# A hybrid attention and DeltaNet layer: ones ahead, the norm row spread by TensorE, key products evicted by ScalarE, three more query pairs in seven products

## The chip, the cores and the metric

The kernel runs on one NeuronCore of a Trainium2 chip. The metric is the device time of one execution in microseconds (us), lower is better. Engines are named as in the profile: PE (TensorE, with PEld for its weight loads), DVE (VectorE), ACT (ScalarE), POOL (GpSimd), SP (SyncE, which issues nearly all DMAs).

## The reference

One decoder layer on 528 tokens (16 meta tokens ahead of 512) of width 1024, f32. One RMS norm feeds one big projection; two branches run beside each other on it, are gated, merged and projected back.

```python
h = concatenate([meta, x])                               # 528 x 1024
hn = rms_norm(h, norm_w)
aq, ak, av, az, dq, dk, dv, dz, db, da, ga, gd = split(hn @ w_in)
# attention branch: 8 heads, two softmaxes each, p0 - lam * p1, causal
y_a = (rms_norm(diff_attention(aq, ak, av)) * silu(az)) @ w_branch_attn
# delta branch: 8 heads; q, k, v by a causal convolution over 4 tokens and silu,
# q and k l2-normalised, gates beta and g, chunks with a triangular solve and a state
y_d = (rms_norm(gated_delta(q, k, v, beta, g)) * silu(dz)) @ w_branch_delta
out = rms_norm(h + (sigmoid(ga) * y_a + sigmoid(gd) * y_d) @ w_out, final_norm_w)[16:]
```

## The kernel before

All matrix products are done in three passes of a split: a value is a high part (rounded to the matmul's type) plus a low part, and high x high, high x low and low x high are summed. So each weight block of 128 output columns is loaded (`raw`, 512 KB), ACT casts its high part (`wh`) and DVE subtracts for the low part (`wl`); the normed input stands as `hnH` and `hnL`, features on partitions, tokens along the free axis.

**Start.** `loads` issues the DMAs on SP's queue: four tiles of x (`xt`, 128 tokens each), the norm row `nwb` broadcast to 128 partitions, the meta tokens (`mt`), and weight blocks between them. `normalise(n)` squares a tile on ACT (the sum is `ss`), DVE multiplies it by the norm row (`weigh`), POOL takes the power -1/2 (`rs`), DVE makes a diagonal `dg` of it, and PE transposes and scales the tile with matmuls against `dg` into PSUM banks; ACT casts to `hnH` and DVE subtracts to `hnL`. `first_products` multiplies the first two key blocks as soon as their tokens are there.

**Middle.** Four groups of two delta heads and two attention heads. `ORDER` (from `dense_order`) lists the weight blocks in the order in which PE takes them: keys, values and queries of the delta heads (dk, dv, dq), their gates (dz), and ak, av, aq, az of the attention heads. A single block takes 48 matmuls, 24 in each of two stretches of tokens, or 24 of 512 columns (`product`). Blocks named in `PAIRS` are taken two at a time (`pair_of_blocks`) by seven products of half size in place of eight (a Strassen-like scheme): sums of weights are built on DVE (`st`, `raw`, in `split_pair`), sums of the input (`sumH`, `sumL`) once at the start. This holds for ak with av, and from the second group for pairs of dk and of dv. After a block come a convolution on DVE (`xp`, `y`), tanh on ACT, and for the delta heads `delta_pair`: key products (`products`, into `MT`), query products (`queries`, into `AT`), a triangular solve (`ts`, `TM`, `square`), a state `S` carried over four chunks (`steps`), and the meta tokens' part of the state (`um`). `attention` does scores and softmax (`psc`, `e`). PSUM is six banks plus a double one `psc`; SLOTS and BANKS say how many buffers of each kind there are.

**End.** The two branch matrices in pairs, then `w_out` in 512-column products; `finish` adds the residual, squares (ACT), multiplies by the final norm row (`fnw`, DVE), takes a power (POOL), scales (ACT for the left half, DVE for the right) and stores. The last tile's right half comes in two pieces of 256.

The order of every engine's instructions is fixed when the program is built: a planner (`Plan`) runs the generators (each `yield` names an engine, an event or a buffer) on costs per instruction, and at each step takes the one that could start first, then the lower rank. `COLD` is the time until which it doubles the cost of PE's work. So an edit in one place moves instructions all over the program; nearly every instruction has source line L231, that of the recording helper, so the profile is read by tiles.

Of the kernel before, what the change touches and what calls it, by code (L numbers as in the profile page):

```python
# [18 lines left out]
P = 128  # L19
# [40 lines left out]
PAIRS = [n for n, (name, i) in enumerate(ORDER) if name == "ak" or name in ("dk", "dv") and i > 1 and i % 2 == 0]  # L60
# [19 lines left out]
COLD = 10500  # L80
# [185 lines left out]
def hybrid_block(ctx: ExitStack, tc: tile.TileContext, x, meta, wblk, wbd, wout, pcol, prow, out):  # L266
# [52 lines left out]
    nwb = mk(sp, [P, D], F32, "nwb")  # L319
# [178 lines left out]
    def loads():  # L498
        for n in range(1, NC + 1):
            yield SP  # L500
            S.dma_start(out=xt[n], in_=x[P * (n - 1):P * n, :])
            done(f"x{n}")
            if n == 1:
                yield SP
                S.dma_start(out=nwb, in_=prow[:, 1296:2320].broadcast_to([P, D]))
                done("nwb")
                yield SP
# [12 lines left out]
        for n in range(2, len(ORDER) + 8):  # L520
            yield from load_weights(n)
# [4 lines left out]
    def normalise(n):  # L526
# [3 lines left out]
        ss, rs, dg = (mk(sp, [P, k], F32, t, 3) for k, t in ((1, "ss"), (1, "rs"), (P, "dg")))  # L530
# [3 lines left out]
        def weigh():  # L534
            yield "nwb"
            yield DVE
            V.tensor_tensor(out=xt[n], in0=xt[n], in1=mt[:, P:2 * P] if n == 0 else nwb, op=ALU.mult)
            done(f"xw{n}")

        spawn(weigh())  # L540
        src = ss
        if n == 0:
# [4 lines left out]
            T.matmul(pt[:, 0:1], samb.rearrange("p k t -> p (k t)"), ss, start=True, stop=True)  # L547
            src = pt[:, 0:1]
# [10 lines left out]
        def part(pt, dst):  # L559
            yield ACT  # L560
            A.copy(out=hn[0][dst], in_=pt)
            tick(f"hh{n}", 1 if n == 0 else 2)
# [5 lines left out]
        for hf in range(1 if n == 0 else 2):  # L568
# [12 lines left out]
            spawn(part(pt, dst))  # L581
# [318 lines left out]

    def after_dq(h, banks):
        pair["q", h], _ = yield from conv_silu(banks, h, NM, "qT")
        give("y")
        done(f"dq{h}")
# [82 lines left out]
    def delta_pair(gi):  # L987
# [114 lines left out]
        def products(i):  # L1102
# [12 lines left out]
            for c in range(NC):  # L1115
                yield DVE
# [134 lines left out]
        yield name("scr")  # L1251
        msub = room[1].rearrange("p a t -> p (a t)")[:, 0:D].rearrange("p (j i) -> p j i", i=32)
# [41 lines left out]
        def meta_state():  # L1294
# [15 lines left out]
            for i in range(2):  # L1310
                yield DVE
                um.append(mk(dp, [32, P], F32, "um", 2))
                V.tensor_scalar_mul(out=um[i], in0=pm[0:32, 0:P], scalar1=ms[:, 4 + i:5 + i])
# [94 lines left out]
        def square(i):  # L1408
# [5 lines left out]
            yield DVE  # L1414
            V.tensor_copy(out=t64[64:128, 4 * i:4 * i + 4], in_=px[64:128])
# [6 lines left out]
            yield DVE  # L1422
            V.tensor_scalar_mul(out=TT[0:64, 4 * i:4 * i + 4, 64:128], in0=py[0:64], scalar1=-1.0)
# [222 lines left out]
    WHOLE = dict(dk=whole_dk, dv=whole_dv, ak=whole_ak, av=whole_av)  # L1646
# [165 lines left out]
    def first_products():  # L1812

        yield ("psc",)
        sc = bank("psc")
        dst = [[], (sc[:, 0, :], sc[:, 1, :])]
        for _ in range(2):
            yield ("pd",)
            dst[0].append(bank("pd"))
        banks = [Banks(n) for n in range(2)]  # L1820
        for hb, (t0, nn) in enumerate(FULL):
            for n in range(2):
                pd = dst[n][hb][:, :nn]
                for m, (i, j) in enumerate(((0, 0), (1, 0), (0, 1))):
                    yield (f"wh{n}", f"w{n}")[i]
                    for e in (0, 1, 2) if hb == 0 else (3, 4):
                        yield f"{('hh', 'hn')[j]}{e}"
                    for k in range(KB):
                        yield PE
# [4 lines left out]
                if hb == 0:  # L1834
                    spawn(after_dk(n, banks[n], ("pd", "pd") if n == 0 else (None, "psc")), 1)
# [172 lines left out]
    def finish(hf, tb, c0, c1, pd, tag, ssq, fnw, xr):  # L2008
# [13 lines left out]
        def weigh():  # L2022
            yield DVE
            V.tensor_tensor(out=t, in0=t, in1=fnw[hf][:, c0:c1], op=ALU.mult)
            tick(f"fw{tb}", 3 if tb == NC - 1 else 2)

        spawn(weigh(), 2)
# [4 lines left out]
        elif c1 == 512:  # L2032
# [7 lines left out]
            def scale(o):  # L2040
                t = xr[o, tb]
                if o == 0:
                    yield ACT
                    A.activation(out=t, in_=t, func=AF.Copy, scale=ssq[:, 4:5])
                else:
# [3 lines left out]
                S.dma_start(out=out[tb * P:(tb + 1) * P, 512 * o:512 * o + 512], in_=t)  # L2049

            for o in range(2):
                spawn(scale(o))
# [93 lines left out]
    for task, rank in ((loads(), 0), (constants(), 5), (gates(), 0.6), (deltas(), 0), (pools(), 0), (dense(), 4),  # L2146
# [53 lines left out]
```

## Time and profile before

| | us |
|---|---|
| median of 3 runs (lowest to highest) | 757.53 (757.01 to 758.4) |
| the profiled execution's own time | 757.24 |
| its span | 755.5 |
| PE busy (instructions) | 735.5 (5311) |
| DVE busy | 626.2 (1431) |
| ACT busy | 498.6 (1322) |
| mean granted clock of TensorE | 0.997 |

Matmuls overlap in the pipeline, so PE's busy time counts the union, and the price of one is read from the distance between starts, not from its duration. In a row of a timeline stand start, duration, engine, operation, output<-inputs, sizes and, in brackets, the idle time of the engine before it and what ended it. In a row of a group stand count, busy time, mean ns of one, and idle time before.

### The profile page before, as it was taken

To read this page: it belongs to the slowest core of one execution; us is meant where nothing else is said; L and a number is where in the kernel's file an instruction comes from. 1 tells how busy PE (TensorE), PEld (TensorE's weight loads), DVE (VectorE), ACT (ScalarE), POOL (GpSimd) and SP (SyncE) were. 2 spreads that over 40 slices of the span, in tenths; PEclk is the share of its full clock that TensorE was granted. 3 is DMA by queue.
4 is the path that set the end of the run, shared out by engine and by line. 5 is a ranking of instruction groups with operands and counts; after the bars stand their busy time and mean duration, and the time that the engine had idled before them with its cause. 6 is when DMAs were issued, how large, how long until landed. Compare 5 with 4: busy or idle time off the path is not lost.

```text
span 755.5 us, 14370 instructions
## 1 busy us (share of the span) xinstructions
PE 735.5 (97%) x5311; PEld 668.6 (88%) x5311; DVE 626.2 (83%) x1431; ACT 498.6 (66%) x1322; POOL 74.7 (10%) x86
## 2 busy tenths in 40 slices
PE   5999999999999999999999999999999999999996
PEld 5998888899899899989989989988988998899875
DVE  6999999998889789879989888997479869797453
ACT  6369565879965678976767797767675445545132
POOL 3205000202000301100030210010000000000001
PEclk9999999999999999999999999999999999999998
DMA  8141321225314112521331152152141443132602
GB/s 306 57 133 33 114 80 64 64 71 158 97 42 140 34 53 85 169 78 52 110 79 59 36 180 85 56 202 65 49 147 57 141 130 121 56 118 90 239 4 109
DMA packets 45431, 74.88 MB, mean 99 GB/s; under 512 B 20728, under 2 KB 25636, under 8 KB 45360
## 3 DMA queue, kind: packets, MB, share of 16 engines
q1 hardware_dynamic: 45360, 73.95, 30.8%
q8 instruction: 42, 0.69, 0.4%
q14 instruction: 29, 0.24, 0.1%
HBM read 67.58 MB, written 6.36 MB: 98 GB/s over the span
## 4 chain that ended last, share of the span: by engine, by line
PE 83%; ACT 8%; DVE 4%; issue 2%; DMA 1%; POOL 0%; SPq 0%; POOLq 0%; ACTq 0%
PE bank L231 80%; PE psc L231 3%; ACT wh L231 2%; DVE wl L231 1%; ACT TM L231 1%; ACT ak L231 1%; DMA xt<-in_x_dram 1%; ACT vr L231 0%; DMA raw<-in_wblk_dram 0%; ACT bank L231 0%; ACT MT L231 0%; ACT e L231 0%; ACT aq L231 0%; ACT sqk L231 0%; DVE hnL L231 0%
## 5 line engine op out<-in xcount | busy, mean ns | idle before, releaser
L231 PE MATMUL bank<-hnH,wh 128*128 128x512 f32 (+4 forms) x664 | 233.4, 355 | 0.7 <-ACT hnH L231 0.7
L231 PE MATMUL bank<-hnH,wl 128*128 128x512 f32 (+4 forms) x664 | 221.6, 337 | 0.0
L231 PE MATMUL bank<-hnL,wh 128*128 128x512 f32 (+4 forms) x664 | 221.5, 337 | 0.0
L231 DVE TENSOR_TENSOR wl<-raw,wh 128x1024 fp32r<-128x1024 f32 (+1 forms) x120 | 134.9, 1126 | 24.6 <-ACT wh L231 24.1
L231 ACT CAST wh<-raw 128x1024 fp32r<-128x1024 f32 (+1 forms) x120 | 116.3, 971 | 43.4 <-PE bank L231 36.0
L231 PEld LDWEIGHTS bank<-hnH,wl 128*128 128x128 f32 x664 | 124.1, 188 | 13.9
L231 PEld LDWEIGHTS bank<-hnH,wh 128*128 128x128 f32 x664 | 124.5, 189 | 13.4 <-ACT hnH L231 0.9
L231 PEld LDWEIGHTS bank<-hnL,wh 128*128 128x128 f32 x664 | 124.4, 189 | 10.0
L231 PE MATMUL bank<-sumH,wh 128*128 128x264 f32 x224 | 68.5, 306 | 0.0
L231 PE MATMUL bank<-sumH,wl 128*128 128x264 f32 x224 | 63.6, 284 | 0.0
L231 PE MATMUL bank<-sumL,wh 128*128 128x264 f32 x224 | 63.5, 284 | 0.0
L231 DVE SCALAR_TENSOR_TENSOR y<-xp,pc,y 128x528 f32<-128x528 f32 (+1 forms) x72 | 54.0, 753 | 1.1 <-ACT y L231 1.0
L231 ACT ACTIVATE e<-psc,ast 128x144 f32<-128x144 f32 (+3 forms) x64 | 34.7, 543 | 21.5 <-DVE ast L231 18.3
L231 PEld LDWEIGHTS bank<-sumH,wh 128*128 128x128 f32 x224 | 42.3, 189 | 1.1 <-issue 0.6
L231 PEld LDWEIGHTS bank<-sumL,wh 128*128 128x128 f32 x224 | 42.4, 189 | 0.0
L231 PEld LDWEIGHTS bank<-sumH,wl 128*128 128x128 f32 x224 | 42.1, 188 | 0.0
L231 PE MATMUL bank<-btH,wh 128*128 128x256 f32 x128 | 36.1, 282 | 0.5 <-ACT sn L231 0.5
L231 PE MATMUL bank<-btH,wl 128*128 128x256 f32 x128 | 35.8, 280 | 0.0
L231 PE MATMUL bank<-btL,wh 128*128 128x256 f32 x128 | 35.8, 280 | 0.0
L231 ACT CAST wh<-st 128x1024 fp32r<-128x1024 f32 x22 | 23.1, 1048 | 13.0 <-PE bank L231 12.8
L231 PE MATMUL psc<-ak,aq 128*128 128x264 f32 (+3 forms) x160 | 29.7, 305 | 0.8 <-DVE aq L231 0.4
L231 DVE TENSOR_TENSOR wl<-st,wh 128x1024 fp32r<-128x1024 f32 x22 | 26.8, 1218 | 3.4 <-ACT wh L231 1.9
(373 smaller groups left out, 1699.5 us busy)
## 6 DMA issues: line engine op xcount, KB each, us to landing
raw<-in_wblk_dram SPq DMA_DIRECT2D x96, 512.0 KB, 3.5
raw<-in_wout_dram SPq DMA_DIRECT2D x8, 512.0 KB, 5.1
xt<-in_x_dram SPq DMA_DIRECT2D x4, 512.0 KB, 4.8
TM<-gcd SPq DMA_DIRECT2D x8, 256.0 KB, 5.2
xr<-in_x_dram SPq DMA_DIRECT2D x8, 256.0 KB, 6.3
out_dram<-xr SPq DMA_DIRECT2D x8, 256.0 KB, 2.5
room<-scrm SPq DMA_DIRECT2D x12, 128.0 KB, 3.3
oad<-room SPq DMA_DIRECT2D x6, 256.0 KB
```

The source lines that it names most:

```text
L231: return real(*args, **kw)
```

## The change

The norm row is loaded as one row (`nrow`, 4 KB, on ACT's queue) and spread over the partitions by PE into two PSUM tiles of 512 columns, in one bank and one half of `psc`, after eight products of ones with ones; two more such products stand behind the meta tokens' sum. `weigh` takes a tile in two halves from these. The first products take their banks later and wait for halves of `hnH`. `products` evicts on ACT with the scale and multiplies by the decay in one DVE instruction of 512 columns; `square` and `um` evict on ACT as well. Query blocks of groups 2 to 4 join `PAIRS`. In groups 2 to 4 the gates (dz) come last, in the first the order of queries, gates and the attention head changes. The last tile is scaled and stored in three pieces, its last 256 columns with weight and scale in one DVE instruction. `COLD` goes from 10500 to 5200, and the triangular solve's input is fetched only once the token sum `t3` is done, whose tile it reuses.

```diff
-        order += k + v + (a0 + q + z[:1] + a1 + z[1:] if g else q + z + a0 + a1)
+        order += k + v + (a0 + q + a1 + z if g else q + a0[2:3] + z[:1] + a0[:2] + a0[3:] + z[1:] + a1)
-PAIRS = [n for n, (name, i) in enumerate(ORDER) if name == "ak" or name in ("dk", "dv") and i > 1 and i % 2 == 0]
+PAIRS = [n for n, (name, i) in enumerate(ORDER) if name == "ak" or name in ("dk", "dv", "dq") and i > 1 and i % 2 == 0]
-COLD = 10500
+COLD = 5200
...
-    nwb = mk(sp, [P, D], F32, "nwb")
+    nrow = mk(sp, [1, D], F32, "nrow")
+    nc.scalar.dma_start(out=nrow, in_=prow[:, 1296:2320])
...
-                S.dma_start(out=nwb, in_=prow[:, 1296:2320].broadcast_to([P, D]))
...
+            for hf in range(2):
+                yield f"norm weights {hf}"
+                yield DVE
+                t = xt[n][:, 512 * hf:512 * hf + 512]
+                V.tensor_tensor(out=t, in0=t, in1=late["nw"][hf], op=ALU.mult)
...
+    def norm_weights():
+        yield ("pdl",)
+        late["nw"] = [bank("pdl")]
+        yield ("psc",)
+        late["nw"].append(bank("psc")[:, 0])
+        yield PE
+        for _ in range(8):
+            T.matmul(late["nw"][0][:, 0:P], ones, ones, start=True, stop=True)
+        yield "nrow"
+        for hf in range(2):
+            yield PE
+            T.matmul(late["nw"][hf], ones[0:1], nrow[:, 512 * hf:512 * hf + 512], start=True, stop=True)
+            done(f"norm weights {hf}")
...
             for c in range(NC):
-                yield DVE
-                V.scalar_tensor_tensor(out=mt[i][:, c, :], in0=pg[:, c], scalar=sc[:, i, c, s_:s_ + 1],
-                                       in1=E_[i][:, c, :], op0=ALU.mult, op1=ALU.mult)
+                yield ACT
+                A.activation(out=mt[i][:, c, :], in_=pg[:, c], func=AF.Copy, scale=sc[:, i, c, s_:s_ + 1])
             give("pdl", pg)
+            yield DVE
+            V.tensor_tensor(out=mt[i], in0=mt[i], in1=E_[i], op=ALU.mult)
...
-                V.tensor_scalar_mul(out=um[i], in0=pm[0:32, 0:P], scalar1=ms[:, 4 + i:5 + i])
+                A.activation(out=um[i], in_=pm[0:32, 0:P], func=AF.Copy, scale=ms[:, 4 + i:5 + i])
...
-            V.tensor_copy(out=t64[64:128, 4 * i:4 * i + 4], in_=px[64:128])
+            A.copy(out=t64[64:128, 4 * i:4 * i + 4], in_=px[64:128])
...
-            V.tensor_scalar_mul(out=TT[0:64, 4 * i:4 * i + 4, 64:128], in0=py[0:64], scalar1=-1.0)
+            A.mul(TT[0:64, 4 * i:4 * i + 4, 64:128], py[0:64], -1.0)
...
+                elif last and a:
+                    yield DVE
+                    V.scalar_tensor_tensor(out=t, in0=t, scalar=ssq[:, 4:5], in1=fnw[o][:, a:b], op0=ALU.mult, op1=ALU.mult)
...
-            for o in range(2):
-                spawn(scale(o))
+            for o, a, b in ((1, 0, 256), (0, 0, 512), (1, 256, 512)) if last else ((0, 0, 512), (1, 0, 512)):
+                spawn(scale(o, a, b))
```

Where this moves instructions: DVE at the start, from the first sum of squares (`ss`) to the first low part of a weight (`wl`). Before:

```order
L231 TENSOR_SCALAR ss_177<-ss_177 128x1
L231 TENSOR_TENSOR xt_122<-xt_122,nwb_84 128x1024
L231 TENSOR_SCALAR dg_179<-ident,rs_178 128x128
L231 TENSOR_TENSOR mt_85<-mt_85 128x128
L231 TENSOR_SCALAR ss_182<-bank_3_80 128x1
L231 TENSOR_SCALAR dg_184<-ident,rs_183 128x128
L231 TENSOR_SCALAR ss_186<-ss_186 128x1
L231 TENSOR_TENSOR xt_123<-xt_123,nwb_84 128x1024
L231 TENSOR_SCALAR dg_188<-ident,rs_187 128x128
L231 TENSOR_TENSOR wl_20_117<-raw_14_111,wh_19_116 128x1024
```

and now:

```order
L231 TENSOR_SCALAR ss_186<-ss_186 128x1
L231 TENSOR_TENSOR xt_123<-xt_123,bank_1_78 128x512
L231 TENSOR_SCALAR dg_188<-ident,rs_187 128x128
L231 TENSOR_TENSOR mt_86<-mt_86 128x128
L231 TENSOR_TENSOR xt_123<-xt_123,psc_176 128x512
L231 TENSOR_SCALAR ss_190<-bank_3_80 128x1
L231 TENSOR_SCALAR ss_194<-ss_194 128x1
L231 TENSOR_TENSOR xt_124<-xt_124,bank_1_78 128x512
L231 TENSOR_SCALAR dg_192<-ident,rs_191 128x128
L231 TENSOR_TENSOR xt_124<-xt_124,psc_176 128x512
L231 TENSOR_SCALAR dg_196<-ident,rs_195 128x128
L231 TENSOR_TENSOR wl_20_118<-raw_14_112,wh_19_117 128x1024
```

The weighting of each x tile reads the two PSUM tiles and stands as two instructions with others between them; what follows keeps its order.

PE at its start, to the first product of a weight block. Before:

```order
L231 MATMUL bank_3_80<-ss_182,samb_96 128x1
L231 MATMUL bank_4_81<-dg_179,xt_122 128x128 x4
L231 MATMUL bank_5_82<-dg_179,xt_122 128x128 x4
L231 MATMUL bank_6_83<-dg_184,mt_85 128x128
L231 MATMUL bank_3_80<-dg_188,xt_123 128x128 x4
L231 MATMUL bank_4_81<-dg_188,xt_123 128x128 x4
L231 MATMUL bank_1_78<-hnH,wh_19_116 128x272 x8
L231 MATMUL bank_1_78<-hnH,wl_20_117 128x272 x3
L231 MATMUL bank_5_82<-dg_193,xt_124 128x128 x4
```

and now:

```order
L231 MATMUL bank_1_78<-ones 128x128 x8
L231 MATMUL bank_1_78<-nrow_84,ones 128x512
L231 MATMUL psc_176<-nrow_84,ones 128x512
L231 MATMUL bank_3_80<-ss_190,samb_97 128x1
L231 MATMUL bank_3_80<-ones 128x128 x2
L231 MATMUL bank_4_81<-dg_188,xt_123 128x128 x4
L231 MATMUL bank_5_82<-dg_188,xt_123 128x128 x4
L231 MATMUL bank_6_83<-dg_192,mt_86 128x128
L231 MATMUL bank_3_80<-dg_196,xt_124 128x128 x4
L231 MATMUL bank_4_81<-dg_196,xt_124 128x128 x4
L231 MATMUL bank_2_79<-hnH,wh_19_117 128x272 x8
L231 MATMUL bank_2_79<-hnH,wl_20_118 128x272 x8
```

The products of ones and the spreading of the row come ahead of everything else, and the first weight block's second pass is no longer broken by the third tile's transposes.

ACT where the keys of the second group arrive (`vr` are values, `TM` the decays, `e` and `ao` attention). Before, with the key products on DVE:

```order
L231 ACTIVATE TM_2116<-TM_2116,gc 128x128
L231 ACTIVATE TM_2116<-TM_2116 128x512
L231 ACTIVATE vr_2458<-bank_1_78,sc_677 128x128
L231 CAST pmT_2452<-bank_4_81 96x128
L231 ACTIVATE vr_2458<-bank_1_78,sc_677 128x128
L231 ACTIVATE e_2409,ast_2407<-psc_2471,ast_2407 128x528
L231 ACTIVATE vr_2458<-bank_1_78,sc_677 128x128
L231 CAST ak_2516<-vT_93_655 64x528
```

and now:

```order
L231 ACTIVATE vr_2486<-bank_6_83,sc_741 128x128
L231 COPY pT_2493<-bank_2_79 128x384
L231 ACTIVATE vr_2486<-bank_6_83,sc_741 128x128
L231 ACTIVATE MT_2504<-bank_1_78,sc_741 128x128
L231 ACTIVATE vr_2486<-bank_6_83,sc_741 128x128
L231 ACTIVATE MT_2504<-bank_1_78,sc_741 128x128
L231 CAST pmT_2494<-bank_4_81 96x128
L231 ACTIVATE MT_2504<-bank_1_78,sc_741 128x128 x2
L231 ACTIVATE e_2447,ast_2445<-psc_2532,ast_2445 128x528
L231 CAST ak_2553<-vT_95_721 64x528
```

The four evictions of a head's key product (`MT`) stand between those of the values and ahead of the attention's exponential and the next keys.

More of the change, by code (lines that the diff above doesn't have):

```diff
@@ L529, in normalise @@
         w = P if n == 0 else D
[L530 removed]
+        ss, rs, dg = (mk(sp, [P, k], F32, t, 5) for k, t in ((1, "ss"), (1, "rs"), (P, "dg")))
         yield ACT
@@ L547, in normalise @@
             T.matmul(pt[:, 0:1], samb.rearrange("p k t -> p (k t)"), ss, start=True, stop=True)
+            for _ in range(2):
+                T.matmul(pt[:, P:2 * P], ones, ones, start=True, stop=True)
             src = pt[:, 0:1]
@@ L899, in whole_dv, with whole_dq @@
         done(f"dv{h}")
+    def whole_dq(h, which):
+        pair["q", h], _ = yield from conv(which, h, NM, "qT")
+        give("y")
+        done(f"dq{h}")
     def after_dq(h, banks):
@@ L1812, in first_products @@
     def first_products():
[L1814 to L1819, printed above, removed]
+        dst = [[], []]
         banks = [Banks(n) for n in range(2)]
@@ L2024, in weigh @@
             V.tensor_tensor(out=t, in0=t, in1=fnw[hf][:, c0:c1], op=ALU.mult)
-            tick(f"fw{tb}", 3 if tb == NC - 1 else 2)
-        spawn(weigh(), 2)
+            tick(f"fw{tb}", 2)
+        last = tb == NC - 1 and hf == 1 and c1 == 512
+        if not last:
+            spawn(weigh(), 2)
         if col == 0:
```

49 lines of the change are left out of this document (32 added, 17 removed).

## The prediction

> **What bounds the kernel now.** I read the page first, then busy time by stretch, then the chain, then the timeline of the first 20 us and the last 8, then the groups by form.
>
> ```profile
> span 755.5 us, 14370 instructions
> PE 735.5 (97%) x5311; PEld 668.6 (88%) x5311; DVE 626.2 (83%) x1431; ACT 498.6 (66%) x1322; POOL 74.7 (10%) x86
> PE 83%; ACT 8%; DVE 4%; issue 2%; DMA 1%; POOL 0%; SPq 0%; POOLq 0%; ACTq 0%
> ```
>
> TensorE (PE) is busy 97% of the span and holds 83% of the chain. The span is 755.5; this execution took 757.24 in all, so 1.7 us lie around it; the median of the runs is 757.53. Below, columns are busy time and instructions of each engine.
>
> ```profile
> core 0: us, PE busy (x) PEld busy (x) DVE busy (x) ACT busy (x) POOL busy (x), PEclk, DMA share, GB/s
> 8.00:12.00 4.00, 3.91 (x19) 3.88 (x19) 2.72 (x8) 3.65 (x7) 2.01 (x2) 1.00 1.03 421
> 12.00:18.00 6.00, 4.94 (x31) 4.51 (x30) 6.00 (x12) 4.57 (x10) 1.46 (x2) 1.00 0.89 314
> 18.00:73.00 55.00, 55.00 (x431) 51.99 (x430) 51.77 (x127) 36.19 (x95) 18.58 (x11) 1.00 0.25 80
> 73.00:81.00 8.00, 7.04 (x42) 5.74 (x41) 8.00 (x16) 4.67 (x15) 0.00 (x0) 1.00 0.09 14
> 81.00:200.00 119.00, 117.38 (x908) 107.69 (x909) 107.04 (x263) 90.13 (x260) 14.30 (x15) 1.00 0.32 98
> 200.00:420.00 220.00, 219.31 (x1728) 202.92 (x1727) 197.88 (x495) 163.87 (x480) 20.33 (x25) 1.00 0.27 80
> 420.00:460.00 40.00, 38.62 (x278) 35.13 (x277) 30.76 (x69) 36.90 (x113) 7.22 (x8) 1.00 0.36 115
> 460.00:744.00 284.00, 283.54 (x1845) 251.23 (x1844) 215.90 (x434) 152.55 (x335) 7.00 (x8) 1.00 0.32 105
> 744.00:755.50 11.50, 5.17 (x45) 4.97 (x43) 3.77 (x11) 3.19 (x8) 1.59 (x2) 0.83 0.25 93
> ```
>
> Between 18 and 744 us PE is idle only 0.0+1.0+1.6+0.7+1.4+0.5 = 5.1 us. So three things can shorten this kernel: less to multiply, an earlier dense start (before 18 us PE runs in pieces), a shorter tail. But VectorE (DVE) is at 90 to 100% in those stretches up to 420 us, so added DVE work has little room.
>
> **Seven products for three query pairs.** Each group's query pair is 96 matmuls of 258 columns now; groups 2 to 4 take 84 of 264, as the pairs of keys and values do. A matmul's own duration overlaps the next, so the price is start to start. First and last of 33 starts in a row; then the step into a stretch, and the first and last of the 29 starts behind it:
>
> ```profile
> 338.37 0.28 PE L231 MATMUL bank<-hnH,wh 128*128 128x258 f32 x1
> ...
> 342.19 0.29 PE L231 MATMUL bank<-hnH,wl 128*128 128x258 f32 x1
> ...
> 82.22 0.37 PE L231 MATMUL bank<-hnH,wh 128*128 128x264 f32 x1
> 82.42 0.29 PE L231 MATMUL bank<-hnL,wh 128*128 128x264 f32 x1
> ...
> 85.84 0.28 PE L231 MATMUL bank<-sumH,wl 128*128 128x264 f32 x1
> ```
>
> 3.82/32 = 0.119 and 3.42/28 = 0.122 us. Three pairs: 288 x 0.119 = 34.4 out, 252 x 0.122 = 30.8 in, 3.6 us saved. A pair has seven products where a wait can break the row, against four, and the step into that stretch (82.22 to 82.42) cost 0.08 more than a plain one: 3 x 3 x 0.08 = 0.7 back. I take **-2.9**, ends -3.6 and -2.2. What it costs elsewhere is summed below.
>
> **Products to ScalarE.** DVE loses the 32 scaled evictions MT<-bank, 16 evictions TM<-bank of 64x256 and 8 um; it gains 8 multiplications of 128x512 (priced like AT) and, for each query pair, four half-size sums, 1.5 more wl and four totals of 264 (priced like TM<-bank).
>
> ```profile
> L231 DVE SCALAR_TENSOR_TENSOR MT<-bank,sc,TM 128x128 f32<-128x128 f32 x32 | 10.5, 340 | 1.2 <-POOL TM L231 1.1
> L231 DVE TENSOR_TENSOR AT<-bank,TM 128x512 f32<-128x512 f32 x8 | 5.5, 682 | 0.0
> L231 DVE COPY TM<-bank 64x256 f32<-64x256 f32 x8 | 3.2, 426 | 0.2
> L231 DVE TENSOR_TENSOR st<-raw 128x512 f32<-128x512 f32 x22 | 15.5, 703 | 2.6 <-DMA raw<-in_wblk_dram 2.6
> L231 ACT ACTIVATE vr<-bank,sc 128x128 f32<-128x128 f32 x32 | 11.6, 367 | 0.4 <-PE bank L231 0.3
> ```
>
> Two stretches in which a new group's keys arrive (columns as above):
>
> ```profile
> 180.00:200.00 20.00, 19.67 (x135) 17.37 (x134) 16.81 (x40) 19.70 (x61) 2.02 (x4) 1.00 0.51 162
> 440.00:460.00 20.00, 19.40 (x120) 16.65 (x119) 17.07 (x28) 19.59 (x45) 1.70 (x2) 1.00 0.48 149
> ```
>
> DVE: -10.5 + 5.5 - 16 x 0.43 - 8 x 0.34 + 3 x (4 x 0.70 + 1.9 + 4 x 0.43) = +4.7 us (1.5 wl at two sums of 0.70 for a full one comes to about 1.9). ScalarE (ACT), by the row vr: 32 x 0.367 + 24 x 0.37 = +20.6, and some 1.3 more for each query pair (1.5 more wh, one eviction fewer; estimated at the same sizes), +24 in all. In the two stretches ACT is busy 98% and DVE 84 to 85%, so eight evictions per group (2.9 us) go onto the fuller engine. What covers that is PE's runway: three slots hold split weights and a 512-column block lasts 24 x 0.23 = 5.6 us, so two ready blocks cover 11 us, and ACT's lateness per group is 2.9 + 1.3. On the path I cost the move at **0**: its ends are -5.1 (every PE wait above goes) and +6 (half of ACT's 12.6 us in three groups is not covered). Gates last in each group is costed at 0: the delta output waits for the second head's gate, which stands last already.
>
> **The start.** The norm row was a 512 KB broadcast between the first and second x tile on SP's queue; now 4 KB go by ACT's queue and PE spreads the row into two PSUM tiles with matmuls against ones, after eight warming ones.
>
> ```profile
> 0.92 0.17 DVE L231 MEMSET ones<- 128x128 f32 x1
> 6.65 1.23 DVE L231 TENSOR_TENSOR xt<-xt,nwb 128x1024 f32<-128x1024 f32 x1 [0.97 <-DMA nwb<-in_prow_dram]
> 8.13 3.78 PE L231 MATMUL bank<-dg,xt 128*128 128x128 f32 x16
> 8.28 1.06 ACT L231 ACTIVATE st<-xt 128x1024 f32<-128x1024 f32 x1 [0.89 <-DMA xt<-in_x_dram]
> 11.39 1.22 DVE L231 TENSOR_TENSOR wl<-raw,wh 128x1024 fp32r<-128x1024 f32 x1
> 14.84 0.75 PE L231 MATMUL bank<-hnH,wh 128*128 128x272 f32 x4
> 17.79 2.05 PE L231 MATMUL bank<-dg,xt 128*128 128x128 f32 x16 [0.40 <-DVE ss L231]
> ```
>
> The second x tile, for which ACT waits until 8.28, and all that is queued behind it come sooner by 512 KB at the 421 and 314 GB/s of 8 to 18 us, 1.2 to 1.7 us. The first tile's weighting need not wait for 6.65 either, but now waits for PE: eight f32 products of ones are 16 passes (each shows as two), which from 1.1 us at 3.78/16 = 0.236 end at 4.9; two passes of 512 columns for a half cost 1.0 us at the later pace (2.05/16 = 0.128 for 128 columns), so the halves stand at 5.9 and 7.0 and the tile is weighted at about 7.7, against 7.88. From there DVE is gapless to 18 us (6.00 of 6.00): with the second tile at 6.8 it reaches the first wl near 9.3 rather than 11.39, and its work to the last hnL is the same but for 0.15 for each later tile in halves. So DVE, and with it the dense start, moves up by 1.5 to 2.1, and PE, which repeats less slowly, by a little more. I take **-2.2**, ends -3.5 (all of PE's slow transposes too) and +1.0: if PE stays at 0.236 while it spreads the row, a half costs 1.9 us, the tile is weighted at 9.4 and the earlier transfers buy nothing.
>
> [...]
>
> **The tail.**
>
> ```profile
> 750.51 0.66 POOL L231 TENSOR_TENSOR ssq<-ssq,mhalf 128x1 f32<-128x1 f32 x1 [4.20 <-DVE ssq L231]
> 751.21 0.72 ACT L231 ACTIVATE xr<-xr,ssq 128x512 f32<-128x512 f32 x1 [0.97 <-POOL ssq L231]
> 751.21 0.49 DVE L231 TENSOR_SCALAR xr<-xr,ssq 128x512 f32<-128x512 f32 x1 [0.44 <-POOL ssq L231]
> ```
>
> The power on POOL ends last (751.17), and the weighting that is removed was beside it. After it DVE does two pieces (about 0.3 and 0.4) in place of one of 0.49 and ACT the same 0.72, so scaling still ends at 751.9. Three stores are issued instead of two, the first some 0.2 sooner, the last one later but half as large. **0**, ends -0.3 and +0.5.
>
> **Sum:** -2.9 + 0 - 2.2 + 0 = -5.1 on 757.24, or 752.4 against the median 757.53. I forecast 752.4; its own range is 749.5 to 755.
>
> **Rivals.** (1) ACT becomes the bound where a group's keys arrive. For it: 98% busy in the two stretches of 20 us, and the chain is on ACT for 8%. Against: PE is busy 97 to 98% in the same rows, so it has a runway. It decides when over 5.1 + 1.5 of ACT's 3 x 4.2 = 12.6 us fall on PE; if all do, 757.5 - 5.1 + 12.6 = 765. (2) DVE gives the query pairs' gain back: +6.3 us of DVE per group, less 3.6 moved away, is +2.7 in three groups where DVE is at 90%; if half of 8.1 lands on PE, 756.5. For it: 73 to 81, where DVE is 8.00 of 8.00 and PE loses 1 us. Against: 200 to 420 has DVE at 90% and PE idle 0.7. (3) The lighter DVE at the triangular solve and the keys removes waits: up to 5.1 more, 748 for some 4.5 of it. (4) PE spreads the row at the slow pace: the start gives nothing, 755. [...]
>
> **Chances.** The forecast 0.48, (3) 0.12, (4) 0.08, (2) 0.17, (1) 0.15. About 0.2% (1.5 us) is what this kernel's runs can tell from no change: faster is below 756.0, slower above 759.0. (2) is same with 0.14 of its 0.17, (1) is slower with 0.14. So faster 0.71, same 0.15, slower 0.14. The range 747 to 760 leaves out some 0.04 below and 0.12 above.
>
> **What would show it.** PE's first 128x272 product near 13 us instead of 14.84 and dense from 16 instead of 18; 96 matmuls of 258 columns left, and 1428 of 264 in place of 1176; PE idle of about 5 us from there to the tail; the power on POOL still the tail's last step. I am wrong if PE's idle time between start and tail passes 8 us, or if the first product starts after 14.5.

## The result and the profile after

The changed kernel takes 751.75 us (median of 4 runs, 751.14 to 753.91) against 757.48 before (4 runs, 757.01 to 758.4): ratio 0.9926, 95% interval 0.9914 to 0.9938. That is 5.7 us less; 5.1 were forecast. The profiled execution took 751.14 with a span of 749.4, 6.1 less than the profiled one before. The first lines of its page:

```profile
span 749.4 us, 14381 instructions
...
PE 735.4 (98%) x5299; PEld 668.8 (89%) x5299; DVE 629.4 (84%) x1417; ACT 516.0 (69%) x1381; POOL 71.8 (10%) x86
```

PE's busy time is the same as before: up to 8 us PE is now busy for 6.86 us instead of 0.55, mostly with products of ones and of the norm row, and behind 18 us for 6.9 us less. DVE rose by 3.2 us (4.7 were worked out), ACT by 17.4 (24 worked out). Busy time by stretch, after; columns as before:

```profile
8.00:12.00 4.00, 4.00 (x22) 3.71 (x21) 2.77 (x6) 3.87 (x7) 0.94 (x2) 0.61 0.97 382
12.00:18.00 6.00, 5.40 (x43) 4.96 (x42) 6.00 (x12) 4.81 (x9) 0.55 (x1) 1.00 0.89 343
18.00:740.00 722.00, 716.00 (x5185) 651.64 (x5184) 615.22 (x1383) 502.06 (x1355) 67.17 (x68) 1.00 0.30 94
```

and the last of these stretches before:

```profile
18.00:740.00 722.00, 716.89 (x5202) 651.38 (x5202) 610.16 (x1395) 483.59 (x1294) 66.71 (x67) 1.00 0.30 94
```

Between 18 and 740 us PE is idle for 722.00 - 716.00 = 6.0 us, and was for 5.1. So the middle isn't shorter because waits went; it is shorter because there is less to multiply. The timeline after: the start, a row of a query pair's matmuls, the tail.

```profile
4.62 1.12 PE L231 MATMUL bank<-nrow,ones 1*128 1x512 f32 x2
5.58 1.02 PE L231 MATMUL psc<-nrow,ones 1*128 1x512 f32 x2
7.00 0.68 DVE L231 TENSOR_TENSOR xt<-xt,psc 128x512 f32<-128x512 f32 x1
7.30 3.23 PE L231 MATMUL bank<-dg,xt 128*128 128x128 f32 x16
8.05 1.06 ACT L231 ACTIVATE st<-xt 128x1024 f32<-128x1024 f32 x1 [1.87 <-DMA xt<-in_x_dram]
10.89 1.22 DVE L231 TENSOR_TENSOR wl<-raw,wh 128x1024 fp32r<-128x1024 f32 x1
13.99 1.38 PE L231 MATMUL bank<-hnH,wh 128*128 128x272 f32 x8
15.21 1.17 PE L231 MATMUL bank<-hnH,wl 128*128 128x272 f32 x8
...
198.28 0.28 PE L231 MATMUL bank<-hnH,wh 128*128 128x264 f32 x1
...
199.61 0.28 PE L231 MATMUL bank<-hnH,wl 128*128 128x264 f32 x1
...
744.51 0.55 POOL L231 TENSOR_TENSOR ssq<-ssq,mhalf 128x1 f32<-128x1 f32 x1 [4.26 <-DVE ssq L231]
745.09 0.72 ACT L231 ACTIVATE xr<-xr,ssq 128x512 f32<-128x512 f32 x1 [0.85 <-POOL ssq L231]
745.36 0.48 DVE L231 SCALAR_TENSOR_TENSOR xr<-xr,ssq,fnw 128x256 f32<-128x256 f32 x1
```

The norm weights stand at 5.7 and 6.6 us, the first x tile is weighted at 7.68, the first 128x272 product starts at 13.99 instead of 14.84, and its rows are no longer broken into fours. The third block's 128x272 products start 2.2 us sooner, which is what the start gave; before, then after:

```profile
36.45 0.29 PE L231 MATMUL bank<-hnH,wh 128*128 128x272 f32 x1
```

```profile
34.21 0.29 PE L231 MATMUL bank<-hnH,wh 128*128 128x272 f32 x1
```

From 198.28 to 199.61 there are 11 steps of 0.121. The power on POOL ends at 745.06, 4.34 ahead of the end of the span; it was 751.17 and 4.33. Groups by form, after (a group, its count, busy time and mean, then PE's waits just ahead of it):

```profile
L231 PE MATMUL bank<-sumH,wh 128*128 128x264 f32 x272 | 82.4, 303 | 0.0
L231 PE MATMUL bank<-hnH,wh 128*128 128x264 f32 x204 | 62.9, 309 | 2.6 <-DVE vT L231 2.1 <-ACT MT L231 0.2 <-DVE xp L231 0.2
L231 PE MATMUL bank<-hnH,wh 128*128 128x258 f32 x32 | 9.5, 296 | 0.0
L231 ACT ACTIVATE MT<-bank,sc 128x128 f32<-128x128 f32 x32 | 10.7, 361 | 0.0
L231 DVE TENSOR_TENSOR MT<-MT,TM 128x512 f32<-128x512 f32 x8 | 5.4, 686 | 1.4 <-ACT MT L231 1.2
```

The forms come in threes (high and low parts): 3 x 32 = 96 matmuls of 258 columns are left, and 3 x (272 + 204) = 1428 of 264. What PE waited for, after (total, times, longest):

```profile
PE bank L231 <- DVE vT L231: 2.1, 3, 0.8
PE bank L231 <- DVE tdmt L231: 0.9, 1, 0.9
PE bank L231 <- ACT sn L231: 0.9, 2, 0.5
PE bank L231 <- ACT pmT L231: 0.6, 2, 0.4
```

No wait passes 1.1 us. Most in total go to totals written to `vT`. These are the totals of the pairs of attention keys and values, which were pairs before too; PE's three waits for them are at 111, 347 and 471 us. At the totals of a query pair (202 to 212, 329 to 338 and 452 to 462 us, written to `xp`) no wait of PE stands in the profile.

### The profile page after: what moved, and what is told of

It is laid out like the page before. It is cut to its first block, busy times and chain, and to the rows that moved or that the text cites. A ratio compares the mean times of both kernels' runs of the same rounds, so it can differ in the third digit from the quotient of the medians.

```text
span 749.4 us, 14381 instructions
## 1 busy us (share of the span) xinstructions
PE 735.4 (98%) x5299; PEld 668.8 (89%) x5299; DVE 629.4 (84%) x1417; ACT 516.0 (69%) x1381; POOL 71.8 (10%) x86
## 4 chain that ended last, share of the span: by engine, by line
PE 71%; ACT 12%; DVE 11%; issue 3%; DMA 2%; SPq 0%; POOL 0%; POOLq 0%; DVEq 0%; ACTq 0%
PE bank L231 68%; DVE wl L231 3%; PE psc L231 2%; ACT wh L231 2%; ACT ak L231 1%; ACT TM L231 1%; DMA raw<-in_wblk_dram 1%; DVE tmps L231 1%; DVE ts L231 1%; DMA xt<-in_x_dram 1%; DVE y L231 1%; DVE raw L231 1%; ACT MT L231 1%; DVE ast L231 1%; ACT vr L231 1%
## 5 line engine op out<-in xcount | busy, mean ns | idle before, releaser
L231 PE MATMUL bank<-hnH,wh 128*128 128x512 f32 (+4 forms) x612 | 218.1, 361 | 2.6 <-DVE vT L231 2.1
L231 PE MATMUL bank<-hnL,wh 128*128 128x512 f32 (+4 forms) x612 | 206.1, 342 | 0.0
L231 PE MATMUL bank<-hnH,wl 128*128 128x512 f32 (+4 forms) x612 | 205.8, 342 | 0.0
L231 PEld LDWEIGHTS bank<-hnH,wh 128*128 128x128 f32 x612 | 114.2, 189 | 16.2 <-DVE vT L231 2.8
L231 PEld LDWEIGHTS bank<-hnH,wl 128*128 128x128 f32 x612 | 113.8, 188 | 13.9
L231 PEld LDWEIGHTS bank<-hnL,wh 128*128 128x128 f32 x612 | 114.2, 189 | 10.0
L231 PE MATMUL bank<-sumH,wh 128*128 128x264 f32 x272 | 82.4, 303 | 0.0
L231 PE MATMUL bank<-sumH,wl 128*128 128x264 f32 x272 | 77.2, 284 | 0.0
L231 PE MATMUL bank<-sumL,wh 128*128 128x264 f32 x272 | 77.1, 283 | 0.0
L231 PEld LDWEIGHTS bank<-sumH,wh 128*128 128x128 f32 x272 | 51.5, 189 | 0.6 <-issue 0.2
L231 ACT ACTIVATE e<-psc,ast 128x144 f32<-128x144 f32 (+3 forms) x64 | 34.5, 540 | 12.5 <-DVE ast L231 11.4
L231 PE MATMUL bank<-btH,wh 128*128 128x256 f32 x128 | 36.6, 286 | 1.0 <-ACT sn L231 0.9
L231 DVE TENSOR_TENSOR wl<-st,wh 128x1024 fp32r<-128x1024 f32 x25 | 30.7, 1229 | 6.2 <-ACT wh L231 6.2
```

The costliest lines, as they stand in the source:

```text
L231: return real(*args, **kw)
```

## The experiments

Three accounts are used for each run. PE's idle time between 18 and 740 us is as above. "First to last" is the time from the start of the first 128x272 product to the start of the last matmul: 734.06 before, 728.90 after. "Broken" is what start-to-start steps there exceed the median step of their form by, counted where it is over 60 ns: 34.95 us before, 33.90 after. All three are of the one profiled execution; the times given first are medians of the runs. The kernel before was run again beside each group of experiments (medians 757.30 to 757.47); the changed kernel was not.

### One part undone, all else as changed, the order planned anew

e1, query pairs in four products:

```diff
-PAIRS = [n for n, (name, i) in enumerate(ORDER) if name == "ak" or name in ("dk", "dv", "dq") and i > 1 and i % 2 == 0]
+PAIRS = [n for n, (name, i) in enumerate(ORDER) if name == "ak" or name in ("dk", "dv") and i > 1 and i % 2 == 0]
```

> The changed kernel with the query pairs of groups 2 to 4 back in four products of 258 columns; all else as changed. Theory A (the sum: three pairs save PE 2.9 to 3.6 us, the start 2.3, the rest is near 0): 751.75 + 2.9 to 3.6 = 754.6 to 755.4 us, that is 2.1 to 2.9 below the kernel before. Theory B (the seven-product pairs give their gain back through VectorE's sums, and the middle became shorter because evictions moved to ScalarE): within 0.7 us of the changed kernel, 751.0 to 752.5. Theory C (the middle's 3.8 us are mostly another order of the same work, which any edit shuffles by 1 to 2 us): anywhere in 752 to 757, with idle time of PE between 18 and 740 us that differs by over 1.5 us from the changed kernel's 5.

Measured: 757.01 us (755.23 to 757.82, 11 runs), ratio to the kernel before 0.9988 (0.9979 to 0.9997), 5.3 above the changed kernel: more than theory A's 3.6, and theory B falls. Theory C's sign, idle time that differs by over 1.5 us, is not there: 7.3 us against 6.0 (the expectation had put 5 for the changed kernel). The profile parts the 5.3 in two. First to last is 733.10, 4.2 above the changed kernel, with the same broken time (33.99): this is the products, 3.8 by rows. The rest is the start, whose code is the same but ran otherwise:

```profile
4.86 2.07 PE L231 MATMUL bank<-nrow,ones 1*128 1x512 f32 x2
6.72 1.91 PE L231 MATMUL psc<-nrow,ones 1*128 1x512 f32 x2
8.67 0.69 DVE L231 TENSOR_TENSOR xt<-xt,psc 128x512 f32<-128x512 f32 x1 [0.62 <-PE psc L231]
10.00 3.30 PE L231 MATMUL bank<-dg,xt 128*128 128x128 f32 x16
15.71 1.27 PE L231 MATMUL bank<-hnH,wh 128*128 128x272 f32 x8 [0.40 <-ACT hnH L231]
```

PE spread the row at half the pace (2.07 and 1.91 against 1.12 and 1.02), the tile was weighted at 9.36, and the first product came at 15.71 instead of 13.99. That is rival (4) of the prediction, with its 1.9 a half and its 9.4. I take it as a matter of the execution, not of the edit, since the start's instructions are the same and the runs differ among themselves: three of this kernel's eleven runs took 755.23 to 755.59, 3.7 above the changed kernel's usual 751.7, at a mean granted clock of 0.997; the eight at 0.999 took 755.73 to 757.82. (The longer ones have the higher mean; in e1's profile the clock's column reads 1.00 while a transposing pass takes 0.21 us, see the last paragraph of this text.) The changed kernel has what look like the same two kinds: 751.14 to 751.82 at 0.997, and one run of 753.91 at 0.999, which was not profiled. Of the eight profiled executions with this start, three spread the row at half the pace: e1, f1 and f3.

e2, the start of before (and the planner's time for it):

```diff
-    nrow = mk(sp, [1, D], F32, "nrow")
-    nc.scalar.dma_start(out=nrow, in_=prow[:, 1296:2320])
+    nwb = mk(sp, [P, D], F32, "nwb")
...
+                S.dma_start(out=nwb, in_=prow[:, 1296:2320].broadcast_to([P, D]))
...
-COLD = 5200
+COLD = 10500
```

> The changed kernel with the start of before: the norm row as one 512 KB broadcast between the x tiles, whole-tile weighting, no products of ones, the first products' banks and waits as before, and the planner's time for the first products back at 10500. Theory A: the start is worth what the traces show at 34 to 36 us, so 751.75 + 2.3 = 754.0 us (753.5 to 754.6), and the middle behind the first products keeps its length. Theory C (luck of the order): over 1 us away from that in either direction. A theory that the earlier start is swallowed by a later transfer (weights then bind): 751.75 to 752.5.

Measured: 760.71 us, ratio 1.0053 (1.0035 to 1.0072): 9.0 above the changed kernel. The start explains 2.2 of it: the third block's products start at 36.45 us, as in the kernel before. The rest comes behind it. From there to the last matmul this run takes 715.1 us and the changed kernel 708.7, with 9.9 us of idle time and 39.8 of broken time. So the middle did not keep its length, as theory A had it.

e3, evictions back on VectorE:

```diff
             for c in range(NC):
-                yield ACT
-                A.activation(out=mt[i][:, c, :], in_=pg[:, c], func=AF.Copy, scale=sc[:, i, c, s_:s_ + 1])
+                yield DVE
+                V.scalar_tensor_tensor(out=mt[i][:, c, :], in0=pg[:, c], scalar=sc[:, i, c, s_:s_ + 1],
+                                       in1=E_[i][:, c, :], op0=ALU.mult, op1=ALU.mult)
...
```

> The changed kernel with the scaled evictions of the keys' products, um, and the two copies of the squaring back on VectorE. Theory A (these moves cost and bring nothing on the path): 751.2 to 752.3 us. Theory B (they make the room that the query pairs' sums take on VectorE, which is at 92 to 100% from 210 to 240, 270 to 290, 330 to 370 and 430 to 500 us): VectorE has 10.5 - 5.5 + 9.6 = 14.6 us more to do, of which a third to a half lands in PE waits: 754 to 757. Rival D (ScalarE, at 95 to 100% from 170 to 200, 280 to 320 and 420 to 440, is what limits there, so that taking the work back frees it): 749.5 to 751.

Measured: 761.44 us, ratio 1.0062 (1.0049 to 1.0075), beyond all three theories. PE's idle time is 11.4 us, broken time 44.1. Its longest waits are of kinds for which the changed kernel waits 0.9 us (`tdmt`) and not at all (`sumL`):

```profile
PE bank L231 <- DVE tdmt L231: 2.8, 2, 2.3
PE bank L231 <- DVE sumL L231: 2.2, 1, 2.2
```

e4, the order of gates in each group as before:

```diff
-        order += k + v + (a0 + q + a1 + z if g else q + a0[2:3] + z[:1] + a0[:2] + a0[3:] + z[1:] + a1)
+        order += k + v + (a0 + q + z[:1] + a1 + z[1:] if g else q + z + a0 + a1)
```

> The changed kernel with the order of before of the gates and values in each group: the first head's gate ahead of the second head's attention blocks, and in the first group both gates ahead of the attention blocks. Theory A: no effect, 751.3 to 752.2 us. Theory C (re-ordering alone moves the middle): off by 1 to 2 us. Theory E (the late gates are what lets the waits for keys and values go): 753 to 754, with one PE wait for a gate or output in each of groups 2 to 4.

Measured: 764.36 us, ratio 1.0096 (1.0072 to 1.0119). No theory had that. Idle time 12.7 us, broken time 43.7; the longest wait, 2.45 us at 90.69, is one for which the profile names no engine.

The four undone parts cost 5.3 + 9.0 + 9.7 + 12.6 = 36.6 us, and the whole change brought 5.7. They can't all be the parts' own worth, to be added up: either the parts lean on each other, or the new order that each edit lets the planner write costs something by itself. In the traces of these four runs some 2000 to 2600 of PE's 5300 instructions stand out of the changed kernel's order.

### The order alone

n2 and n3 change one number that only the planner reads:

```diff
-    HOP = {PE: 200, DVE: 130, ACT: 140, POOL: 90, SP: 0}
+    HOP = {PE: 205, DVE: 130, ACT: 140, POOL: 90, SP: 0}
```

> The changed kernel with one number of its planner changed, which no instruction depends on: the time it reckons from a product of TensorE to who waits for it is 205 ns, not 200. From the first quarter on this writes another order (730 of TensorE's rows stand elsewhere); the work is the same. Theory P (the 5 to 12 us that each undone part cost in the first four runs are mostly the price of leaving this one order, and hardly the parts'): 754 to 760 us, PE waits of over 1 us somewhere between 60 and 480 us. Theory Q (any order that the planner writes is as good, so that the undone parts really cost 5 to 12 us): 751 to 752.7.

> The same with 195 ns in place of 200: another order from about a third on (542 of TensorE's rows). Theory P: 753 to 760, and not the same as with 205. Theory Q: 751 to 752.7.

Measured: 759.38 us with 205 (ratio 1.0025, 1.0008 to 1.0042) and 754.27 with 195 (0.9966, 0.9955 to 0.9977). The same instructions in another order (some 1700 and 1000 of PE's stand elsewhere) cost 7.6 and 2.5 us at the median. Theory Q falls. Theory P's ranges hold both times, which shows that an order alone can cost that much, not that the undone parts cost little. With 205 the runs spread: three took 755.75 to 756.34 (mean clock 0.996 to 0.999), four 759.08 to 759.40 (0.991 to 0.992, the profiled one among them) and five 760.86 to 762.42 (0.992 to 0.994). At their median the whole gain is gone, though in the profiled one the first product starts at 13.25, sooner than in the changed kernel. Idle time is 10.8 us, and a wait of PE has a sequel; the wait in the timeline, then busy time by stretch (the figure behind POOL's count is the granted clock):

```profile
384.34 0.40 PE L231 MATMUL bank<-vrm,tdmt 32*32 32x128 f32 x2 [2.15 <-DVE tdmt L231]
```

```profile
380.00:386.00 6.00, 3.85 (x38) 3.25 (x36) 4.92 (x9) 5.87 (x15) 2.34 (x4) 1.00 0.18 33
386.00:394.00 8.00, 8.00 (x60) 7.48 (x58) 3.93 (x9) 5.80 (x16) 0.00 (x0) 0.57 0.31 111
394.00:400.00 6.00, 6.00 (x103) 5.38 (x102) 2.78 (x5) 4.70 (x12) 1.01 (x1) 1.00 0.01 4
```

Behind the wait of 2.15 us the granted clock falls to 0.50: a mean of 0.57 over 8 us is 2 x 0.43 x 8 = 6.9 us at half, which by my estimate costs half of that, 3.4, more (in e3 steps of 264 columns are 0.22 us at 0.50, from 82.60 us on, and 0.12 ahead of the wait). So this run's 8.0 us of span over the changed kernel are 4.8 of added idle time and 3.4 of half clock, less 0.7 at the start, plus some 0.5 of smaller breaks. In e3 the same sum is 5.4 of idle time and 3.4 of half clock (6.8 us of it, behind waits that end at 82.4 and 386.3 us), less 0.4: 8.4 of its 8.6.

### One part undone or done alone, the order of all else held

For these runs the planner followed a recorded list of which task each step belongs to. The edit shown is that of f1, g1, g3 and f9, where what the list lacks was put in by time; in f3 and f2 the place in the list went ahead of time in the planner's comparison, and what the list lacks came first. The traces show how far the order was held: in g3 every instruction of PE stands where it stood, in f3 all but nine, in f9 all but the four that its edit changes.

```diff
-                key = max(t, self.free[eng]), task.rank
+                key = max(t, self.free[eng]), task.rank
+                place = PLACE.get(self.label(task))
+                if place is not None:
+                    if held is None or place < held[0]:
+                        held = place, key, task
+                    continue
```

f3 is e3's edit in the changed kernel's order:

> The keys' products, um and the copies of the squaring back on VectorE as in the third of the first runs, but every engine's order of the rest held as in the changed kernel (the planner follows the changed kernel's recorded list). Theory P: the undone moves alone are worth little, 751.5 to 754, since VectorE's +14.6 us lie beside PE's runway. Theory Q (VectorE needs the room): 757 to 761, as in the run without the held order.

Measured: 759.33 us, ratio 1.0018 (1.0008 to 1.0028), 7.6 above the changed kernel. The profiled execution (760.34) had the slow pace at the start (first product 15.90, 1.9 later). Idle time is 11.3 us, 5.3 more, and PE's new waits are for what the moved evictions feed:

```profile
PE bank L404 <- DVE AT L404: 1.7, 1, 1.7
PE bank L404 <- DVE vin L404: 1.2, 2, 0.7
PE bank L404 <- DVE MT L404: 0.9, 1, 0.9
PE bank L404 <- DVE TM L404: 0.9, 2, 0.6
```

So in this order the evictions on VectorE cost 5 us of waits with the place of everything else unchanged; theory P's 751.5 to 754 fell for them, and theory Q's 757 to 761 holds the time. How much of the 5 us is VectorE's lack of room, and how much an order that was made for ScalarE, this run does not part; g3 below is the same move the other way round, and costs too.

f2 is e2's edit in the changed kernel's order:

> The start of before (norm row broadcast as 512 KB between the x tiles, weighting by whole tiles, no products of ones) with the order of all else held as in the changed kernel. Theory P with the sum: 751.75 + 2.3 = 754.0 (753.5 to 755). Theory Q: 759 to 760.5, as in the run without the held order. A rival for the start itself (nothing of it reaches the end): 751.5 to 752.5.

Measured: 759.92 us, ratio 1.0029 (1.0018 to 1.004). The list did not fit the old start:

```profile
24.91 1.51 PE L404 MATMUL bank<-hnH,wbs 128*32 128x272 f32 x8 [3.08 <-DVE wbs L404]
...
41.66 0.29 PE L404 MATMUL bank<-hnH,wh 128*128 128x272 f32 x1
```

A wait of 3.08 us, and a mean clock of 0.66 from 25 to 30 us behind it. So this run doesn't give the start's own worth. But it shows two other things. PE reaches the third block at 41.66 us, 7.5 behind the changed kernel, and from there to the last matmul takes 708.4 us, as the changed kernel does (708.7): in the held order the middle keeps its length, so the 6.4 us that e2 lost there go with its new order, not with its start. And the span is 7.2 us longer: what is lost ahead of the third block reaches the end nearly in full.

f1 is e1's edit in the changed kernel's order. g1 and g3 put one part alone into the kernel before, in the order of before. g1, query pairs in seven products:

```diff
-PAIRS = [n for n, (name, i) in enumerate(ORDER) if name == "ak" or name in ("dk", "dv") and i > 1 and i % 2 == 0]
+PAIRS = [n for n, (name, i) in enumerate(ORDER) if name == "ak" or name in ("dk", "dv", "dq") and i > 1 and i % 2 == 0]
```

g3, evictions by ScalarE:

```diff
-                yield DVE
-                V.scalar_tensor_tensor(out=mt[i][:, c, :], in0=pg[:, c], scalar=sc[:, i, c, s_:s_ + 1],
-                                       in1=E_[i][:, c, :], op0=ALU.mult, op1=ALU.mult)
+                yield ACT
+                A.activation(out=mt[i][:, c, :], in_=pg[:, c], func=AF.Copy, scale=sc[:, i, c, s_:s_ + 1])
...
```

> The changed kernel with the query pairs of groups 2 to 4 back in four products, the order of all else held as in the changed kernel. The sum (seven products for three pairs save PE 3.6 us of products, nothing is given back since evictions were moved): 751.75 + 3.6 = 755.4 (754.7 to 756). Rival R (VectorE gives the pairs' gain back even in the changed kernel): 751.3 to 753. Over 757 would say that the held order doesn't fit four products.

> The kernel before with one part alone: query pairs of groups 2 to 4 in seven products, the order of all else held as before. The sum: 757.4 - 2.9 = 754.5 (753.8 to 755.3). Rival R (without the evictions moved away, VectorE has 9.6 us more in stretches where it was at 90% already, and PE waits for it): 757 to 760, with PE waits at or behind the pairs' totals. The run with evictions back on VectorE in the held order (759.3) speaks for R.

> The kernel before with one part alone: the keys' products, um and the squaring's copies leave by ScalarE, the order of all else held as before. The sum (0): 756.8 to 758. Rival U (it takes away VectorE waits by itself; VectorE -15, ScalarE +21): 752 to 755. Rival V (ScalarE, at 98% where keys arrive, becomes the bound): 759 to 763, PE waits for ScalarE's casts at 170 to 200, 290 to 320 and 430 to 450.

Measured: f1 768.54 us (ratio 1.0148, 1.0129 to 1.0168), g1 788.10 (1.0397, 1.0384 to 1.0411), g3 766.92 (1.0122, 1.0095 to 1.0149). All are outside every range; only f1's last sentence, on what over 757 would mean, fits. An order made for one kind of products doesn't carry the other: f1 has 16 us of idle time, with waits of up to 3.2 us for weights at 595 to 608 us. In g1 PE runs into waits such as these. The first is for a query, which now comes from a pair that ends later than the old order has it; the second is for attention's exponential, and what delayed that is not shown:

```profile
227.76 2.08 PE L413 MATMUL bank<-qT,kT 128*128 128x128 f32 x8 [3.88 <-DVE qT L413]
...
497.79 1.25 PE L413 MATMUL psc<-ak,aq 128*128 128x264 f32 x4 [3.63 <-ACT e L413]
```

Its idle time from 18 to 740 us is 27.0 us, with a granted clock of 0.50 in three places (near 228, 362 and 496 us, 23.8 us in sum). That is the misfit's size, and no measure of what VectorE gives back; rival R isn't decided by it. g3 has 4.4 us more idle time than the kernel before and 10.2 us at 0.50 (5.1 more, estimated as for n2), which make 9.5 of its 9.9 us of added span.

### The norm row over all rows of the array

f9 is the changed kernel in its own order, with one edit:

```diff
-    nrow = mk(sp, [1, D], F32, "nrow")
-    nc.scalar.dma_start(out=nrow, in_=prow[:, 1296:2320])
+    nrow = mk(sp, [P, D], F32, "nrow")
+    nc.vector.memset(nrow, 0.0)
+    nc.scalar.dma_start(out=nrow[0:1], in_=prow[:, 1296:2320])
...
-            T.matmul(late["nw"][hf], ones[0:1], nrow[:, 512 * hf:512 * hf + 512], start=True, stop=True)
+            T.matmul(late["nw"][hf], ones, nrow[:, 512 * hf:512 * hf + 512], start=True, stop=True)
```

> The changed kernel in its own order, except that the norm row is spread by products over 128 rows (the row on the first partition of a zeroed tile) instead of over one row; one clearing of 128x1024 by VectorE is added ahead. The profile of the changed kernel shows the granted clock at 0.50 from 8 to 10 us, just behind the one-row products, and another execution in which the early products stayed slow to 13 us. Theory W (one-row products leave the array too idle for the clock): no 0.50 at 8 to 11 us, transposes of the first x tile at 0.11 to 0.12 us a pass instead of 0.20, first 128x272 product up to 1 us sooner, 750.7 to 751.7, and the later executions at 753.9 gone. Rival (the clock doesn't ask for the rows used): 751.5 to 752.5, the 0.50 still there; the row lands later by the clearing (0.6 us), which may cost up to 0.5.

Measured: 751.55 us (751.09 to 752.17, 5 runs), ratio 0.9919 (0.9907 to 0.9931): the changed kernel's time. Busy time from 8 to 11 us, with the granted clock behind POOL's count, in f9 and then in the changed kernel:

```profile
8.00:11.00 3.00, 2.94 (x26) 2.69 (x24) 2.98 (x11) 2.22 (x3) 1.07 (x2) 1.00 1.00 399
```

```profile
8.00:11.00 3.00, 3.00 (x14) 2.73 (x13) 1.77 (x6) 2.87 (x5) 0.94 (x2) 0.50 1.00 399
```

and f9's timeline there:

```profile
6.27 1.10 PE L416 MATMUL bank<-nrow,ones 128*128 128x512 f32 x2 [1.45 <-DMA nrow<-in_prow_dram]
8.73 1.95 PE L416 MATMUL bank<-dg,xt 128*128 128x128 f32 x16
13.61 0.75 PE L416 MATMUL bank<-hnH,wh 128*128 128x272 f32 x4
```

As theory W has it, the 0.50 is gone and the 16 transposes take 1.95 us instead of 3.23. The time, which lies in theory W's range and in the rival's, stays: the row's products start 1.65 us later (the row is fetched behind a clearing of 0.91), and the first product, 0.4 sooner, is broken again. None of the five runs is at 753.9; with one in four so in the changed kernel, that is too few to tell. The mean clocks of the four runs without a profile are 0.997, 0.998, 0.999 and 0.999, so a drop in one or two of them is not ruled out.

## Why the prediction was right, point by point

**The sum, 5.1 against 5.7.** The span went from 755.5 to 749.4. At the third block PE is 2.2 us ahead; from there to the last matmul it gains 3.8; the tail gives nothing. Neither sign of being wrong came: PE's idle time is 6.0 us and not over 8, the first product starts at 13.99 and not after 14.5, both in the profiled execution; one that spreads the row at half the pace, as e1's, starts it at 15.71.

**Query pairs, forecast -2.9 (ends -3.6 to -2.2).** 288 matmuls of 258 columns went and 252 of 264 came, as counted. The profile after shows median steps of 0.120 and 0.122: 34.6 - 30.7 = 3.8 us, and the middle gained 3.8. That the two agree so well is partly luck. Counted by form, broken time rose by 3.6 us in the weight blocks' products of 264 columns (14.1 to 17.7) and fell by 1.1 in those of 258, so 2.5 were given back where 0.7 was forecast; it fell by 3.6 in all other rows, 1.7 of that in the 128x272 products at the start. In sum it went from 34.95 to 33.90. e1 took 4.2 us of the products' stretch back with the same broken time in sum (33.99). So the products' 3.8 are shown, by their count, their steps and e1; that the breaks come out even is a net, which no run takes apart.

**The start, -2.2.** 2.2 by the third block's products, and f2 shows that time lost there reaches the end. The path was partly another. The earlier second x tile, on which the term was worked out (6.8 us), came at 8.05 in this execution against 8.28, and the first wl at 10.89 rather than 9.3; the first product came at 13.99, not near 13. This execution is the latest of its kind: ACT starts on that tile at 6.18 (e1) to 8.05 us in the nine traces with the new start, 7.17 in the middle one, and at 8.27 to 8.38 in the five with the old one. So the tile does come about as much sooner as forecast, but with a spread of 1.9 us where the old start has 0.1. Nor does it decide alone: in n2 and n3 the first product starts at 13.25 and 13.31 and the third block only at 34.04 and 33.95. The rest goes with unbroken rows: PE's first products run in rows of 8, 8 and 7 from 13.99 to 17.1, where transposes used to cut in at 17.79 behind 8 and 3. The first tile's transposes took 3.23 us instead of 3.78, so they saved 0.55.

**Evictions to ScalarE, 0, and gates last, 0.** In the result these zeros are right only as a net: PE waits as much as before. As statements about each part they are not shown. f3 has the evictions worth 5 us of waits in this order, g3 has them cost 9.5 us in the order of before; each order was made for the evictions where they stood. For the gates there is only e4, in which a new order is mixed in, and n2 shows that a new order alone can cost 7.6. What the two are worth by themselves stays open, as does a pair's cost on VectorE without the moved evictions.

**The tail, 0.** 4.34 against 4.33 us behind the power on POOL.

**The rivals.** (1), ACT the bound: ACT is indeed at 20.00 of 20.00 from 420 to 440 us, but PE is too; it fell. (2), VectorE gives the gain back: at the query pairs' own totals PE has no wait. New are three waits on VectorE, 2.1 us in all, for the totals of attention's pairs, one of them in the first group, which has no query pair; older waits went, and the sum stayed. (3), waits removed: 5.1 us of idle time became 6.0. (4), the row spread at the slow pace, happens in some executions: three of eight profiled ones with this start, and by its time and clock one of the changed kernel's four runs, about 2.2 us.

The forecast lacked one thing: it took the order of the middle as given. That the planner's new order came out as good as the old one, 6.0 us of idle time against 5.1, was luck: n2 and n3, the same work with one constant of the planner moved by 5 ns, came out 7.6 and 2.5 us worse. The range to 760 covers their medians, but by other causes.

## What to carry to other kernels

Where a planner writes the order, price the bound engine's own work by start-to-start steps, and keep a separate term for a new order: here a 5 ns change of one of its constants moved the same work by 2.5 and 7.6 us. Undoing a part then measures the part and a new order together; run a neutral edit beside it, and trust the part only where idle and broken time came out about equal, as in e1. Holding a recorded order helped here where the edit left alone who waits for whom (f9, and f2 behind its start); where products or evictions changed hands (f1, g1, g3) it brought waits of its own.

## What the runs showed of the hardware

**Behind some waits of TensorE the clock was low.** Waits of 2.15 (n2), 2.16 and 2.31 (e3), 2.26 (f1) and 3.08 us (f2) were each followed within 2.2 us by a granted clock of 0.50, for 3.4 us or, in n2, 6.8. Others were not: one of 2.45 us in e4's profile, one of 3.22 in f1's, one of 1.70 in f3's. And the clock also fell without one: in g3 at 143 and 273 us, with no wait over 0.6 us in the 10 us before, and in g1 at 493 us, 0.9 behind a wait of 1.01. So in these runs the length of one wait does not decide it alone.

**Behind products of one row the clock or the pace was low.** With PE busy without a break from 1.14 us, the changed kernel fell to 0.50 about 1 us behind four one-row passes, which end at 5.58 + 1.02 = 6.60, and e3, e4, n2 and n3 fell like it, all at 7.5 to 7.7 us by their means of 0.88 to 0.93 from 6 to 8 us; e1, where these passes ran from 4.86 to 8.6 us, had slow transposes until 13 (3.30 us for 16 passes), and f1 and f3 were like it (4 instructions of PE from 6 to 8 us in all three, 14 in the changed kernel). With 128 rows (f9) neither was seen in its profile (1.00 from 8 to 11 us, 1.95 us for 16 passes). That rows count for it is suggested by these nine profiles, not shown: f9's passes also come 1.65 us later, behind 1.45 us of idle time, and only one execution of it was profiled.

**The granted-clock column does not show e1's slow start.** It reads 1.00 in e1 from 8 to 13 us, where a transposing pass takes 3.30/16 = 0.21 us, and 0.50 in the changed kernel from 8 to 11, where a pass takes 3.23/16 = 0.20; in f9 it reads 1.00 from 8 to 11, where a pass takes 1.95/16 = 0.12.
